# An up projection as one sequence of 77 products, with weight splits three products ahead and the convolution in pieces

## The chip, the core and the metric

The kernel runs on one NeuronCore of a Trainium2 chip. The metric is the device time of one execution in microseconds (us). "The time before" is the median of three executions; the profile is of one further execution. Engines are called as in the profile: PE is TensorE (PEld its weight loads), DVE is VectorE, ACT is ScalarE, POOL is GpSimd, SP is SyncE, which here only issues DMAs.

## The reference

One layer of a hybrid model on 512 tokens of width 1024: a mixer, a cross attention over 256 memory rows, and a feed-forward block with a short causal convolution. The change lies in the feed-forward block:

```python
def causal_dwconv(x, w, b):          # w has 3 taps here
    k_w = w.shape[0]
    s = x.shape[1]
    xp = jnp.pad(x, ((0, 0), (k_w - 1, 0), (0, 0)))
    y = b
    for j in range(k_w):
        y = y + xp[:, j:j + s] * w[j]
    return y

def conv_ffn(x, w_up, conv_w, conv_b, w_down):
    u = causal_dwconv(x @ w_up, conv_w, conv_b)
    gate, val = jnp.split(u, 2, axis=-1)
    return (jax.nn.gelu(gate) * val) @ w_down

def reference(x, mem, ...):
    ...
        x = layer_norm(ALPHA * x + mix, ln1_g[l], ln1_b[l])
        ca = memory_cross_attention(x, mem, ca_wq[l], ca_wkv[l], ca_wo[l])
        x = layer_norm(ALPHA * x + ca, ln2_g[l], ln2_b[l])
        ff = conv_ffn(x, ffn_w_up[l], ffn_conv_w[l], ffn_conv_b[l], ffn_w_down[l])
        x = layer_norm(ALPHA * x + ff, ln3_g[l], ln3_b[l])
```

`x @ w_up` is 512 x 1024 by 1024 x 5632; the 5632 outputs are 22 pairs of a gate tile and a value tile of 128 each.

## The kernel before

**Products.** Every float32 product is made of three matmuls (`mm3`, lines 154 to 157): each operand is split into a high half (`wh`, cast to fp32r on ACT, L125) and a low half (`wl`, the difference, on DVE, L126), and high x high, high x low and low x high are summed in PSUM. `split` (L119) makes both halves of 128 x 1024 weights, in four rotating `wh` and four rotating `wl` buffers.

**The up projection** goes by 11 "quads" (`quad`, L870) of two pairs each. A quad is a 2 x 2 block product of tokens (two halves of 256) by inputs (two halves of 512) and is done by Winograd's form of Strassen with seven products instead of eight. Each of them (`product`, L863) has 24 matmuls of 128 x 128 by 128 x 256. The token side (`forms`: A11, A12, S1 to S4, A22) is made once by `forms_block` (L794) for each of the four token blocks b, from transposes on PE (L801) and sums and splits on DVE and ACT; blocks 0 and 1 give A11 and A12 alone, the others need blocks 2 and 3 too. The weight side of a quad is made by DMA (`up_forms`, L844): blocks B11, B21, B22 are loaded on the SP queue (L851, L856), and sums are made by accumulating DMAs on the POOL queue (L848): B22 += B12; T1 = B11 + B12 (a load and an accumulation); B11 += the sum in B22; B21 += the sum in B11. B11, B21 and B22 are split as they are first, then added to, and the results are split again. Seven slots of 128 x 1024 hold these blocks.

From the third quad the order of products in a quad is S4 (of B22), A11 (B11), A12 (B21), S3 (B22 + B12), S2 (B11 + that), S1 (T1), A22 (B21 + that). Some PSUM results are kept by an ACT copy (L880: m1, m3, m7, u2), then added on DVE to a later bank (`put`, L884) into `uu`. When a quad's products are done its convolution follows for both pairs: per tile one `Identity` with bias and scale on ACT (L918) and two taps on DVE (L920), a Gelu on ACT (L922) and a multiply on DVE (L923) into `hf`.

**Around it.** The attention's output projection ends in a `slab` (L159, called at L824) that works block by block; `ln2_evict` (L819) adds the residual (L664, statistics L666), normalises (L670, L427, L677, L679) and returns the transposes of the block before. The first two quads begin with the products of A11 and A12 (L925 to L931): A11 and A12 of quad 0, then the transposes of block 3, then A11 and A12 of quad 1. Behind the up projection come two slabs of the down projection, whose left operand is split by `h_split` (L939).

**What sets the order.** Only the kernel's head is scheduled by hand (L279). Everywhere else a scheduler at build time puts the instructions into the in-order queues of the engines: an instruction goes when its inputs and a buffer are free by the scheduler's own reckoning, and among those that are free the one that stands first in the program text.

Of the kernel before, what the change touches and what calls it, by code (L numbers as in the profile page):

```python
# [40 lines left out]
def hybrid_block_kernel(  # L41
# [117 lines left out]
    def slab(xh, xl, w, c0, nk, evict, blocks=NB, late=0, mid=None, mid_k=4, halves=False, pre=None):  # L159
# [659 lines left out]
    def ln2_evict(b, ps):  # L819
        resid(b, ps, 512, 1024)  # L820
        norm(b)
        return lambda: forms_block(b)

    x2_last = slab(tok(oTh), tok(oTl), ca_wo[0], 512, KT, ln2_evict, late=4)  # L824
# [7 lines left out]

    hf = [raws[2]] + [H8(F32, "hf") for j in range(5)]
# [5 lines left out]
    blocks = [q2.tile([P, 1024], F32, name="rawx")]  # L839
    for _ in range(3):  # L840
        r = wp.tile([P, 2048], F32, name="raw", tag="raw", bufs=3)
        blocks += [r[:, 0:1024], r[:, 1024:2048]]

    def up_forms(q, order):  # L844
        blk = lambda kh, ch: ffn_w_up[q, kh, ch]
        at = {n: blocks[(4 * q + i) % 7] for i, n in enumerate(order + ("T1",))}
        r1, r2, r3, r4 = (at[n] for n in ("B11", "B22", "B21", "T1"))
        load, add = nc.sync.dma_start, lambda d, s_: nc.gpsimd.dma_start(d, s_, accum_op=OP.add)  # L848
        src = {"B11": blk(0, 0), "B22": blk(1, 1), "B21": blk(1, 0)}
        for n in order:  # L850
            load(at[n], src[n])  # L851
        for n in order:
            yield split(at[n], (8, P), 16)
            if n == "B22":
                add(r2, blk(0, 1))
        load(r4, blk(0, 0))  # L856
        add(r4, blk(0, 1))
        add(r1, r2)
        add(r3, r1)
        for r in (r2, r1, r4, r3):  # L860
            yield split(r, (8, P), 16)

    def product(bank, n, u, first, last):  # L863
        (h, l), (fh, fl) = u, forms[n]
# [5 lines left out]
    def quad(q):  # L870

        early = q < 2
        us = up_forms(q, ("B11", "B21", "B22") if early else ("B22", "B11", "B21"))
        uu = (hf[3 + q] if early else raws[q % 2]).rearrange("p (c j t) -> p c j t", c=2, j=2)
        g2 = lambda t: t.rearrange("p (j t) -> p j t", j=2)
        t1, t2_ = slice(0, 256), slice(256, 512)

        def kept(bank, name):
            t = t2(name)
            A.copy(t, bank)  # L880
            return g2(t)

        def put(dst, bank, other):
            V.tensor_tensor(dst, g2(bank), other, op=OP.add)  # L884

        def third():
            b = mx_bank()
            product(b, "S4", next(us), True, True)
            return kept(b, "m3")

        if not early:
            m3 = third()
        bp = mm_bank()
        product(bp, "A11", next(us), True, False)
        m1 = kept(bp, "m1")
        b = mx_bank()
        product(b, "A12", next(us), True, True)
        put(uu[:, 0, :, t1], b, m1)
        if early:
            yield  # L900
            m3 = third()
        b4 = mm_bank()
        product(b4, "S3", next(us), True, False)
# [25 lines left out]
    for g in early:  # L929
        for _ in g:  # L930
            pass  # L931
# [71 lines left out]
```

## Time and profile before

| | us |
|---|---|
| median of three executions | 874.77 (873.73 to 875.7) |
| profiled execution | 872.24 |
| its span, first to last instruction | 870.5 |
| PE busy | 806.2 (93%) |
| PEld busy | 709.3 (81%) |
| DVE busy | 570.4 (66%) |
| ACT busy | 376.3 (43%) |
| POOL busy | 68.3 (8%) |

Matmuls are pipelined, so a busy PE need not be a PE at its rate: the distance between the starts of two matmuls tells the rate. An engine's idle time counts only where a chain that sets the end goes through it. In the rows below, "x" is a count, and what stands in square brackets or after `<-` in a timeline is idle time before the instruction and what ended it.

### The profile page before, as it was taken

Reading aid. Unit: us, or ns where it says so; the run is one execution under the profiler, and the core shown is the slowest. Engines: PE = TensorE matmul, PEld = TensorE weight load, DVE = VectorE, ACT = ScalarE, POOL = GpSimd, SP = SyncE. Lnnn points to the kernel's source line nnn. Section 1 sums busy time; section 2 is a strip of 40 time slices with the busy share of each in tenths; the row PEclk is TensorE's granted clock in tenths of the full one; section 3 lists DMA queues with packets and bytes.
Section 4 is the critical chain, followed back from the end, with each engine's and each line's share of the span. In section 5 each row is a group of like instructions: output and inputs, shape, how many; then the busy total and the mean of one; then the engine's idle time right before and its main releaser. Section 6 shows DMA issues by size and latency. Waiting matters only on the chain. (4 is left out here: it accounts for less than half of the span.)

```text
span 870.5 us, 11772 instructions
## 1 busy us (share of the span) xinstructions
PE 806.2 (93%) x4696; PEld 709.3 (81%) x4696; DVE 570.4 (66%) x944; ACT 376.3 (43%) x512; POOL 68.3 (8%) x96
## 2 busy tenths in 40 slices
PE   9979999999999999999995778888898788999996
PEld 7858877787798888889884778888898788888885
DVE  6463498898783893385596377776666768934227
ACT  2289543553252052273152355555544557721110
POOL 1000001001100000000000111101111110000001
PEclk9989999999999999999998788999989899999999
DMA  9936742353257142313401777677686866422202
GB/s 263 184 75 168 105 77 45 91 125 105 79 203 258 48 145 98 97 63 132 121 2 25 184 191 161 158 174 172 152 187 171 194 150 161 173 97 97 73 1 98
DMA packets 53183, 111.05 MB, mean 128 GB/s; under 512 B 3844, under 2 KB 21380, under 8 KB 53128
## 3 DMA queue, kind: packets, MB, share of 16 engines
q1 hardware_dynamic: 46208, 84.58, 33.4%
q0 software_dynamic: 6336, 23.07, 14.3%
q10 hardware_dynamic: 584, 2.64, 0.9%
q8 instruction: 37, 0.61, 0.3%
q14 instruction: 18, 0.15, 0.1%
HBM read 96.63 MB, written 2.12 MB: 113 GB/s over the span
## 5 line engine op out<-in xcount | busy, mean ns | idle before, releaser
L126 DVE TENSOR_TENSOR wl<-raw,wh 128x1024 fp32r<-128x1024 f32 x155 | 187.4, 1221 | 172.3 <-ACT wh L125 171.6
L125 ACT CAST wh<-raw 128x1024 fp32r<-128x1024 f32 x155 | 161.7, 1051 | 311.3 <-PE mm L157 126.2
L157 PE MATMUL mm<-xf,wl 128*128 128x256 f32 x440 | 133.0, 303 | 32.2 <-DVE wl L126 32.1
L155 PE MATMUL mm<-xf,wh 128*128 128x256 f32 x440 | 133.4, 304 | 8.9 <-ACT wh L125 8.1
L156 PE MATMUL mm<-xf,wh 128*128 128x256 f32 x440 | 131.0, 299 | 0.0
L157 PEld LDWEIGHTS mm<-xf,wl 128*128 128x128 f32 x440 | 93.0, 211 | 35.0 <-DVE wl L126 35.0
L155 PEld LDWEIGHTS mm<-xf,wh 128*128 128x128 f32 x440 | 93.1, 212 | 11.4 <-ACT wh L125 8.7
L156 PEld LDWEIGHTS mm<-xf,wh 128*128 128x128 f32 x440 | 92.9, 211 | 0.0
L156 PE MATMUL mm<-wl,hTh 128*128 128x512 f32 (+1 forms) x180 | 65.9, 366 | 0.0
L155 PE MATMUL mm<-wh,hTh 128*128 128x512 f32 (+1 forms) x180 | 65.8, 366 | 0.0
L157 PE MATMUL mm<-wh,hTl 128*128 128x512 f32 (+1 forms) x180 | 65.8, 365 | 0.0
L155 PE MATMUL mm<-wh,xTh 128*128 128x512 f32 x128 | 52.5, 410 | 0.4 <-DVE xTh L285 0.4
L156 PE MATMUL mm<-wl,xTh 128*128 128x512 f32 x128 | 52.0, 406 | 0.0
L157 PE MATMUL mm<-wh,xTl 128*128 128x512 f32 x128 | 51.5, 402 | 0.0
L155 PE MATMUL mm<-xTh,wh 128*128 128x512 f32 x128 | 51.2, 400 | 0.0
L157 PE MATMUL mx<-xf,wl 128*128 128x256 f32 x176 | 49.4, 280 | 1.9 <-DVE wl L126 1.9
L156 PE MATMUL mm<-xTl,wh 128*128 128x512 f32 x128 | 51.1, 399 | 0.0
L157 PE MATMUL mm<-xTh,wl 128*128 128x512 f32 x128 | 51.0, 398 | 0.0
L156 PE MATMUL mx<-xf,wh 128*128 128x256 f32 x176 | 49.5, 281 | 0.8 <-DVE xf L247 0.8
L155 PE MATMUL mx<-xf,wh 128*128 128x256 f32 x176 | 49.9, 284 | 0.2 <-ACT wh L125 0.2
L920 DVE SCALAR_TENSOR_TENSOR fc<-xfr,ncols,fc 128x511 f32<-128x511 f32 (+1 forms) x36 | 25.0, 748 | 24.1 <-ACT fc L918 24.1
L155 PEld LDWEIGHTS mm<-wh,hTh 128*128 128x128 f32 x180 | 34.0, 189 | 5.6
(312 smaller groups left out, 1764.0 us busy)
## 6 DMA issues: line engine op xcount, KB each, us to landing
raw<-in_ffn_w_up_dram SPq DMA_DIRECT2D x37, 512.0 KB, 4.5
raw<-in_w_in_dram SPq DMA_DIRECT2D x14, 1024.0 KB, 8.4
raw<-in_ffn_w_down_dram SPq DMA_DIRECT2D x10, 1024.0 KB, 5.1
raw<-in_ffn_w_up_dram POOLq DMA_DIRECT2D x19, 512.0 KB, 8.6
raw<-in_ca_wkv_dram SPq DMA_DIRECT2D x8, 1024.0 KB, 5.3
raw<-raw POOLq DMA_DIRECT2D x15, 512.0 KB, 4.7
raw<-in_w_out_dram SPq DMA_DIRECT2D x4, 1024.0 KB, 8.9
raw<-in_ca_wq_dram SPq DMA_DIRECT2D x4, 1024.0 KB, 5.0
```

The lines of the kernel that those rows point to most:

```text
L125: A.copy(hv, src)
L126: V.tensor_sub(lv, src, f32(hv))
L155: T.matmul(ps, ah, bh, start=first, stop=False, skip_group_check=True)
L156: T.matmul(ps, ah, bl, start=False, stop=False, skip_group_check=True)
L157: T.matmul(ps, al, bh, start=False, stop=last, skip_group_check=True)
L920: V.scalar_tensor_tensor(f[:, d:], u[:, :S - d], w(2 - d), f[:, d:], op0=OP.mult, op1=OP.add)
```

## The change

The generators `quad` and `up_forms` are replaced by a list `seq` of 77 products (M1 to M7 stand for the forms A11, A12, S4, A22, S1, S2, S3) and a function `step` that places one of them. All six M1 and M2 products of quads 0 to 2 come first, then the others of quads 0 to 2 with the M3 of quad 3 among them, and from quad 3 on M1, M2, M7, M6, the next quad's M3, M5, M4. A step first places the PSUM copies and additions of the product before (`posts`), then the split of the product three places on (`split_of`) with the accumulating DMAs that follow from it, then loads that are due (`AHEAD`), then the 24 matmuls, then one of five pieces of a convolution. There are nine slots for weight blocks instead of seven, taken from a list of free ones; quad 0 has a spare block T3 = B22 + B12 with a load of its own. The first loads are placed inside the slab before (`ffn_begin`), the first three splits ahead of the last block's residual, the transposes of blocks 2 and 3 after the first and third steps. The first three splits of the down projection, each with its `h_split`, stand in the last three steps, and the remaining convolution pieces between the later units of that slab; the load of the last norm's weights moves from `mid_k` 4 to 12. The scheduler still chooses the order in the queues.

```diff
-    def slab(xh, xl, w, c0, nk, evict, blocks=NB, late=0, mid=None, mid_k=4, halves=False, pre=None):
+    def slab(xh, xl, w, c0, nk, evict, blocks=NB, late=0, mid=None, mid_k=4, halves=False, units=None):
...
-        for u in slab_units(w, c0, nk):
+        for u in units or slab_units(w, c0, nk):
...
-            if pre:
-                pre(k0)
...
+    h8 = [H8(F32, "hf") for j in range(5)]
+    hf = [raws[2]] + h8[1:] + h8[:1]
...
+    slots, free = [], list(range(9))
+
+    def ffn_begin():
+        half = lambda t: [t[:, 0:1024], t[:, 1024:2048]]
+        rt = [half(wp.tile([P, 2048], F32, name="raw", tag="raw", bufs=3)) for _ in range(3)]
+        slots[:] = rt[1] + rt[2] + [q2.tile([P, 1024], F32, name="rawx")] + rt[0] + half(hf[5])[::-1]
+        for q in range(3):
+            loads(q, ["B11", "B21"])
+        load(take(0, "T3"), blk(0, "B22"))
+        add(at(0, "T3"), blk(0, "B12"))
+        loads(0, ["B22"])
...
+    FORM = {"M1": "A11", "M2": "A12", "M3": "S4", "M4": "A22", "M5": "S1", "M6": "S2", "M7": "S3"}
+    seq = [(n, q) for q in range(3) for n in ("M1", "M2")]
+    seq += [(n, int(q)) for n, q in (w.split(".") for w in
+            "M3.0 M7.0 M6.0 M3.1 M5.0 M4.0 M3.2 M7.1 M6.1 M3.3 M5.1 M4.1 M7.2 M6.2 M5.2 M4.2".split())]
+    for q in range(3, NQ):
+        seq += [(n, q) for n in ("M1", "M2", "M7", "M6")] + [("M3", q + 1)] * (q + 1 < NQ) + [("M5", q), ("M4", q)]
...
+    def first_t(q):
+        loads(q, ["T1"])
+        add(at(q, "T1"), blk(q, "B12"))
+
+    def split_of(i):
+
+        n, q = seq[i]
+        src = {"M1": "B11", "M2": "B21", "M3": "B22", "M4": "B21", "M5": "T1", "M6": "B11", "M7": "B22"}[n]
...
+        units[i] = split(at(q, src), (8, P), 16)
+        t3 = "T3" if (q, "T3") in held else "B22"
+        if n == "M1":
+            if (q, t3) in held and (q, "summed") in units:
+                add(at(q, "B11"), at(q, t3))
+        if n == "M2":
+            if (q, "summed") in units:
+                add(at(q, "B21"), at(q, "B11"))
+        if n == "M3":
+            units[q, "summed"] = True
+            if t3 == "B22":
+                add(at(q, "B22"), blk(q, "B12"))
+            else:
+                drop(q, "B22")
+            if q not in (1, 2):
+                first_t(q)
+            if q < 3:
+                add(at(q, "B11"), at(q, t3))
+                add(at(q, "B21"), at(q, "B11"))
...
+    def conv_pieces(q):
+        y = {}
+
+        def taps(c, j):
...
+            A.activation(f, u, AF.Identity, bias=col(FCB + ft), scale=w(2))
+            if j:
+                A.activation(y[c, 0], y[c, 0], AF.Gelu_apprx_tanh)
+            for d in (1, 2):
+                V.scalar_tensor_tensor(f[:, d:], u[:, :S - d], w(2 - d), f[:, d:], op0=OP.mult, op1=OP.add)
+            y[c, j] = f
+
+        mul = lambda c: V.tensor_mul(hslice(2 * q + c), y[c, 0], y[c, 1])
+        return [lambda: taps(1, 0), lambda: taps(1, 1), lambda: (mul(1), taps(0, 0)), lambda: taps(0, 1),
+                lambda: mul(0)]
+
+    def step(i):
...
+        for f in posts:
+            f()
+        posts.clear()
+        if i + 3 < len(seq):
+            split_of(i + 3)
+        elif i + 3 - len(seq) < len(down_first):
+            down_first[i + 3 - len(seq)]()
+
+        for m, names in AHEAD.get(i, ()):
...
+        product(b, i, n in ("M1", "M2", "M3", "M7"), n in ("M2", "M3", "M4", "M5"))
+        if pieces:
+            pieces.pop(0)()
...
+    for q in range(1, NQ):
+        if q > 2:
+            AHEAD.setdefault(max(where["M3", q] - 8, 1), []).append((q, ["B22"]))
+            AHEAD.setdefault(where["M1", q] - 7, []).append((q, ["B11", "B21"]))
+    for i, w in ((3, (1, ["B22"])), (6, (2, ["B22"])), (7, (1, "T1")), (12, (2, "T1"))):
+        AHEAD.setdefault(i, []).append(w)
...
+    def ln2_evict(b, ps):
+        if b == NB - 1:
+            for i in range(3):
+                split_of(i)
+        resid(b, ps, 512, 1024)
+        norm(b)
+        return (lambda: forms_block(b)) if b < 2 else None
+
+    slab(tok(oTh), tok(oTl), ca_wo[0], 512, KT, ln2_evict, late=4, mid=ffn_begin)
+    step(0)
+    forms_block(2)
+    step(1)
+    step(2)
+    forms_block(3)
+    for i in range(3, len(seq)):
+        step(i)
...
     slab(tok(hTh), tok(hTl), ffn_w_down[0], 0, NPAIR, lambda b, ps: resid(b, ps),
-         mid=lambda: ln_load(ln3_g, ln3_b), pre=h_split)
+         mid=lambda: ln_load(ln3_g, ln3_b), mid_k=12, units=down_units())
```

## Rows read from the trace of the kernel before

**Rows 1.** The page, section 2: tenths of TensorE's granted clock in 40 slices

```profile
PEclk9989999999999999999998788999989899999999
```

**Rows 2.** Table of stages: length, busy time, granted clock, DMA share and rate

```profile
core 0: us, PE busy (x) PEld busy (x) DVE busy (x) ACT busy (x) POOL busy (x), PEclk, DMA share, GB/s
451.17:521.39 70.22, 51.13 (x347) 48.28 (x346) 43.22 (x60) 29.55 (x41) 8.79 (x10) 0.83 0.52 122
...
521.39:742.51 221.12, 193.18 (x1515) 189.44 (x1513) 158.40 (x193) 122.20 (x159) 29.39 (x34) 0.92 0.71 169
742.51:870.50 127.99, 120.88 (x596) 102.48 (x594) 63.81 (x89) 29.55 (x31) 3.69 (x4) 0.98 0.25 87
```

**Rows 3.** Timeline of PE in the third quad: start, duration, line, operation, tiles

```profile
527.85 0.28 PE L155 MATMUL mx<-xf,wh 128*128 128x256 f32 x1
...
529.55 0.28 PE L155 MATMUL mm<-xf,wh 128*128 128x256 f32 x1
...
533.01 0.58 PE L157 MATMUL mm<-xf,wl 128*128 128x256 f32 x1 [3.07 <-DVE wl L126]
```

**Rows 4.** Waits in the nine late quads: total us, times, longest

```profile
PE mm L157 <- DVE wl L126: 27.3, 9, 4.5
DVE fc L920 <- ACT fc L918: 27.2, 9, 4.4
...
DVE wl L126 <- ACT wh L125: 16.3, 15, 2.2
```

**Rows 5.** Timeline of DVE in the third quad

```profile
526.46 2.78 DVE L920 SCALAR_TENSOR_TENSOR fc<-hf,ncols,fc 128x511 f32<-128x511 f32 x4 [3.02 <-ACT fc L918]
...
530.42 1.40 DVE L920 SCALAR_TENSOR_TENSOR fc<-hf,cols,fc 128x510 f32<-128x510 f32 x2
531.74 1.22 DVE L126 TENSOR_TENSOR wl<-raw,wh 128x1024 fp32r<-128x1024 f32 x1
```

**Rows 6.** Timeline of ACT in the third quad

```profile
524.65 1.05 ACT L125 CAST wh<-raw 128x1024 fp32r<-128x1024 f32 x1 [3.37 <-DMA raw<-in_ffn_w_up_dram]
525.61 1.52 ACT L918 ACTIVATE fc<-hf,cols,ncols 128x512 f32<-128x512 f32 x2
```

**Rows 7.** Timeline of DVE at the opening of the up projection

```profile
449.97 1.22 DVE L126 TENSOR_TENSOR wl<-rawx,wh 128x1024 fp32r<-128x1024 f32 x1
...
452.84 0.68 DVE L811 TENSOR_TENSOR xfr<-mx,xfr 128x512 f32<-128x512 f32 x1
453.44 0.68 DVE L813 TENSOR_TENSOR xfr<-xfr 128x512 f32<-128x512 f32 x1
```

**Rows 8.** Timeline of PE at the opening: the transposes of blocks 2 and 3

```profile
450.38 1.03 PE L801 MATMUL mx<-ident,xres 128*128 128x128 f32 x8
...
463.02 1.64 PE L801 MATMUL mx<-ident,xres 128*128 128x128 f32 x8 [3.08 <-DVE xres L679]
```

**Rows 9.** DMA view of the late quads: queues' shares; issues, median us to landing

```profile
q0 software_dynamic: 5016, 18.25, 44.2%
q1 hardware_dynamic: 6022, 18.89, 26.7%
...
raw<-raw POOLq DMA_DIRECT2D x13, 512.0 KB, 4.7
```

**Rows 10.** DMA view of 610 to 622 us, four issues together

```profile
raw<-in_ffn_w_up_dram SPq DMA_DIRECT2D x2, 512.0 KB, 9.6
raw<-in_ffn_w_up_dram POOLq DMA_DIRECT2D x2, 512.0 KB, 9.4
```

**Rows 11.** DMA view of 472 to 479 us, one accumulation from DRAM

```profile
raw<-in_ffn_w_up_dram POOLq DMA_DIRECT2D x1, 512.0 KB, 5.7
```

**Rows 12.** Timeline of POOL in a late quad

```profile
598.69 0.87 POOL L848 DMA_DIRECT2D rawx<-raw  x1 [8.93 <-issue]
...
610.67 0.85 POOL L848 DMA_DIRECT2D raw<-in_ffn_w_up_dram  x1 [5.97 <-DMA raw<-in_ffn_w_up_dram]
```

**Rows 13.** Timeline of DVE beside that issue

```profile
609.36 2.36 DVE L126 TENSOR_TENSOR wl<-raw,wh 128x1024 fp32r<-128x1024 f32 x2
```

More of the change, by code (lines that the diff above doesn't have):

```diff
@@ L844, in up_forms @@
[L844 to L861, printed above, removed]
@@ new lines, in hybrid_block_kernel, with take, drop, loads @@
+    held, units = {}, {}
+    def take(q, n):
+        ok = [f for f in free if not (q >= NQ - 2 and 5 <= f < 7) and not (q >= 7 and f == 8)]
+        held[q, n] = ok[0]
+        free.remove(ok[0])
+        return slots[ok[0]]
+    at = lambda q, n: slots[held[q, n]]
+    def drop(q, n):
+        free.append(held.pop((q, n)))
+    def loads(q, names):
+        for n in names:
+            load(take(q, n), blk(q, n if n != "T1" else "B11"))
+    def first_t(q):
+        loads(q, ["T1"])
+        add(at(q, "T1"), blk(q, "B12"))
@@ L865, in product @@
+    def product(bank, i, first, last):
+        (h, l), (fh, fl) = units.pop(i), forms[FORM[seq[i][0]]]
         for j in range(2):
@@ L868, in product @@
                     first and j == 0 and k == 0, last and j == 1 and k == 3)
[L870 to L903, printed above, removed]
-        m7 = kept(b4, "m7")
-        product(bp, "S2", next(us), False, False)
-        u2 = kept(bp, "u2")
-        product(bp, "S1", next(us), False, True)
-        put(uu[:, 1, :, t1], bp, m3)
-        put(uu[:, 1, :, t2_], bp, m7)
-        product(b4, "A22", next(us), False, True)
-        put(uu[:, 0, :, t2_], b4, u2)
-        for c in (1, 0):
-            y = []
-            for j in range(2):
-                ft = j * NPAIR + 2 * q + c
-                u, f = uu[:, c, j, :], t2("fc")
-                w = lambda i: ncols[:, i * 44 + ft:i * 44 + ft + 1] if c else col(FCW + i * 44 + ft)
-                A.activation(f, u, AF.Identity, bias=col(FCB + ft), scale=w(2))
-                for d in (1, 2):
-                    V.scalar_tensor_tensor(f[:, d:], u[:, :S - d], w(2 - d), f[:, d:], op0=OP.mult, op1=OP.add)
-                y.append(f)
-            A.activation(y[0], y[0], AF.Gelu_apprx_tanh)
-            V.tensor_mul(hslice(2 * q + c), y[0], y[1])
@@ L925, in hybrid_block_kernel, with keep, put @@
-    early = [quad(q) for q in range(2)]
-    next(early[0])
-    x2_last()
-    next(early[1])
-    for g in early:
-        for _ in g:
-            pass
-    for q in range(2, NQ):
-        for _ in quad(q):
-            pass
+    banks, kept, uus, posts, pieces = {}, {}, {}, [], []
+    g2 = lambda t: t.rearrange("p (j t) -> p j t", j=2)
+    def keep(q, name, bank):
+        t = t2(name)
+        A.copy(t, bank)
+        kept[q, name] = g2(t)
+    def put(q, c, half, bank, name):
+        V.tensor_tensor(uus[q][:, c, :, half * 256:(half + 1) * 256], g2(bank), kept[q, name], op=OP.add)
@@ L950, in h_split, with down_unit, down_units @@
         V.tensor_sub(hTl[j][:, s], hf[j][:, s], f32(hTh[j][:, s]))
+    down = slab_units(ffn_w_down[0], 0, NPAIR)
+    early_units = []
+    def down_unit():
+        h_split(2 * len(early_units))
+        early_units.append(next(down))
+    down_first = [down_unit] * 3
+    def down_units():
+        yield from early_units
+        for k in range(6, NPAIR, 2):
+            h_split(k)
+            if pieces:
+                pieces.pop(0)()
+            yield next(down)
+    def ln2_evict(b, ps):
[13 more added lines that the diff above has]
+        step(i)
+    for f in posts:
+        f()
     slab(tok(hTh), tok(hTl), ffn_w_down[0], 0, NPAIR, lambda b, ps: resid(b, ps),
-         mid=lambda: ln_load(ln3_g, ln3_b), pre=h_split)
+         mid=lambda: ln_load(ln3_g, ln3_b), mid_k=12, units=down_units())
     def ln3_evict(b, ps, cs):
```

56 lines of the change are left out of this document (44 added, 12 removed).

## The prediction

> **What bounds the kernel now.** I read the page's slices first, then the stages, then one product, then the queues that it waits for. In the slices of 21.8 us, the digit of TensorE's clock is below 9 in the third and then only in slices 22 to 25, 30 and 32, which all lie in the up projection, the stage that the change rewrites [rows 1]. The table of stages gives its size: 70.22 us for the first two quads (14 products) and 221.12 us for the other nine (63 products), with a mean granted clock of 0.83 and 0.92, a mixture of the two levels 1.2 and 2.4 GHz; the down projection behind it runs at 0.98 [rows 2].
>
> What would the stage cost without waits? In an undisturbed product, fifteen matmuls take 529.55 - 527.85 = 1.70 us, 0.1133 us each, so a product of 24 takes 2.72 us [rows 3], a quad of seven 19.0 us, and 77 products 209.4 us. The stage takes 291.3 us, so 81.9 us are lost: 221.1 - 63 x 2.72 = 49.7 us in the nine late quads (5.5 us each) and 70.2 - 38.1 = 32.1 us in the opening.
>
> The late loss sits at one place. The fourth product of a quad (S3) starts two matmuls and then stops for `wl`, the low half of its split: in the quad shown for 3.07 us [rows 3]; over the nine quads TensorE waits there 27.3 us, in nine stops [rows 4]. The remaining 22.4 us are mostly matmuls at the lower clock behind each such stop. Why is that `wl` late? On DVE it starts at 531.74, behind seven convolution taps and a multiply, the first of which began at 526.46 [rows 5]; `wh` of the same split was already cast at 524.65, after 3.37 us in which ACT stood at the head of its queue for a DMA, with the four `Identity` operations of the convolution behind it [rows 6]. So ACT waits for the accumulated block B22 + B12, the convolution of the quad before waits for ACT, and the split waits for the convolution. DVE is not short of time as such: 158.4 of 221.1 us, 17.6 us a quad [rows 2].
>
> **The change, part by part.** *Convolution in pieces, splits three products ahead.* Instructions are the same in number. Removed is the order: the convolution of quad q stood in the text ahead of the S3 split of quad q+1; now each step first places the PSUM evictions, then the split of the product three on, then one fifth of the convolution. Four `wh`/`wl` buffers let that split start when the product before the present one has ended, and it must be done three products later: 8.16 us, of which it needs 1.05 + 1.22 us [rows 5, 6]. So 5.9 us are in hand. The whole convolution costs DVE 8 x 0.67 + 2 x 0.60 = 6.6 us (four taps in 2.78 us [rows 5], multiplies at the 0.60 us spacing of [rows 7]), one piece 1.3 to 1.9 us. What hides the convolution is TensorE's own products; without that cover it costs what it costs now, 5.5 us a quad. The scheduler may still let pieces run ahead of a split that is not ready; a whole burst of 6.6 us exceeds what is in hand by only 0.7 us.
>
> *DMAs moved.* Per quad there are, as before, four loads on SP and four accumulations on POOL (plus one load for a spare block in quad 0). Together they hold the sixteen DMA engines 44.2 + 26.7% of 221.1 us, 17.4 us a quad, some of it early down weights [rows 9]; this is under 19.0. What matters is the order on POOL, an in-order queue: B22 += B12 now stands five steps (13.6 us) ahead of its split, formerly three, so the wait at ACT goes. Behind it on POOL stands T1 += B12, which waits for T1's load; behind that B11 += B22 and B21 += B11. The chain that closes on itself is: split of M3 (2.3 us), B22 += B12 lands, B11 += B22 lands, split of M6, and 1 us later the next M3's split on the same queues. The first addition lands in 5.7 us when little else moves [rows 11] and 9.4 us when four issues crowd [rows 10], the second in 4.7 us [rows 9]: a period of 13.7 to 17.4 us, hidden under 19.0 by at least 1.6. SP's queue gains no wait that lasts: following the list of free slots through the sequence, nearly every load goes into a slot whose last reader is three or more steps old (in the first quads a load of B22 and one of T1 wait for a split just placed).
>
> *Opening.* All six products that need the first two token blocks alone now run before the first that needs blocks 2 and 3 (formerly three, and TensorE stopped 3.08 us for the last block's normalisation [rows 8]). From 450.38 TensorE has 6 x 2.72 + 2 x 0.79 us (the eight transposes of [rows 8], until 451.17) = 17.9 us of work, to 468.3. DVE has, from 449.97 to the seventh product: 7 splits x 1.14 [rows 13] and 21 operations of 0.60 us (one residual, four passes of the norm, nine and five for the forms, two evictions) [rows 7], with about 1.2 us (estimate) of small ones: 21.8 us, to 471.8, and about 1 us for hand-overs. So the seventh product starts near 472.8, 4.5 us late; with 2.5 us for the low clock behind it (22.4 / 9) and 1.6 us of transposes the opening costs 8.6 us over pure products. Bounds of the stop: 0, if splits slip ahead of 449.97, and 10, if the norm is again scattered among the forms.
>
> *First quads.* M3 of quads 0 to 3 come only three products apart, so their additions crowd on POOL: three a quad, 5.7 + 4.7 + 4.7 = 15.1 us if alone, 18.8 at the crowded landing. They fit in 16.3 us or miss by 2.5 a quad; the bounds are 0 and 15 us, I take 5, nearer the lone addition.
>
> *Late quads.* 55 products, 7.86 quads, lose between 0 and today's 5.5 us each. I take 0.8, near zero since the split has 5.9 us in hand: 6.3 us. ACT's copy of `u2` now has the next quad's M3 beside it.
>
> *Down projection.* Its first three splits and `h_split`s move into the last three steps; each unit has 24 matmuls of cover, and the bound is 0 to 3 us. I take 0.
>
> Sum: 450.38 + 209.4 + 8.6 + 5 + 6.3 = 679.7 instead of 742.51, 62.8 us earlier. The profiled execution took 872.24 us (1.7 over its span of 870.5): 809.4. The median of the three runs is 2.5 us above that execution, so I forecast **812**.
>
> **A rule weighed.** While DVE ran two splits back to back from 609.36 [rows 13], POOL issued an addition at 610.67 in 0.85 us; with DVE idle, at 598.69, it took 0.87 [rows 12]. So POOL was not held up. The Trainium skill, "SBUF — State Buffer", section "SBUF: two separate sides", says that a DVE operation with two SBUF inputs can hold a port pair against a GpSimd operation that reads SBUF for its whole length; the trace disagrees for these issues. As a mechanism here: each of the two additions of the chain would wait for one 1.22 us split, the period would be 17.4 + 2.4 = 19.8 us, 0.8 over the products, some 8 us on ten rounds: 820. I give it 0.03.
>
> **The rivals.** (a) *DVE becomes the bound.* It has 17.6 of 19.0 us to do, and today it waits for ACT 27.2 us before taps and 16.3 us before `wl` [rows 4], 4.8 us a quad. From a third of this on it is the bound (19.2); if all of it stays, its period is 22.4: 3.4 x 7.86 = 26 us less the 6 counted, 832. Against it: half of the waiting is the DMA wait at ACT that goes.
>
> (b) *The pieces do not stay pieces.* The scheduler is free in its order and the change does not do what it says: the burst still stands ahead of a split, and 5.5 us a quad stay: 43 - 6 = 37 us more, 849. Against it: splits now come ahead in the text, where ties are decided.
>
> (c) *No change*, if DMA and order together restore both losses: 0.03.
>
> (d) *Slower: T1's addition ahead of B22's on POOL.* If the free order puts T1 += B12 first, the chain begins with T1's load. At the crowded landings this is 9.6 + 9.4 + 4.7 + 1 = 24.7 us a round [rows 9, 10], eleven rounds from 472.8, and 5.4 us of products behind: 750, 7.4 us later than now, and with the first quads' 5 us 12.4 later: 887. It decides from a period of 23.6 us, (742.5 - 5.4 - 472.8 - 5) / 11. With the addition uncrowded (5.7) it is hidden as long as the load lands within 7.6 us (7.6 + 5.7 + 4.7 + 1 = 19.0). For it: the opening's crowding; against it: B22's addition is earlier in the text and its wait is shorter.
>
> **How the numbers follow.** Forecast 0.56 (800 to 822; all free, 798), port rule 0.03, (a) 0.14, (b) 0.15, (c) 0.03, (d) 0.09. For 8 in 10 the range goes from 798 to 850. Its lower end is the sum with the opening's stop, first quads and late quads near their lower bounds. What a measurement can tell from no change is about 0.2%, 1.7 us: faster 0.88, same 0.03, slower 0.09.
>
> **What would show it.** Right: the wait of `mm L157` for `wl` shrinks from 27.3 us to a few, the clock of the late quads is near 1.00, a quad takes 19 to 20 us, DMA engines are busy over 80% there, and the seventh product starts within a few us of 472. Wrong: a stop at the same place in every quad, with taps ahead of `wl` on DVE (b); DVE without idle time while TensorE waits (a); ACT waiting for a DMA at M6's cast, with POOL held by T1's load (d).

## The result, and the profile after

The changed kernel takes 827.97 us (median of four runs, 824.04 to 830.77), the kernel before, run beside it, 875.24 us: a ratio of 0.9459, 95% interval 0.9417 to 0.9501. Forecast were 812 us and a range of 798 to 850. The direction was right, and so was the mechanism in the main; the time is 16 us above the forecast and lies between the forecast's own range (800 to 822) and rival (a).

The profiled execution took 830.77 us. Its stages, in the columns of [rows 2]: the first 22 products, the next 49 (seven quads), the last six, the down projection.

```profile
core 0: us, PE busy (x) PEld busy (x) DVE busy (x) ACT busy (x) POOL busy (x), PEclk, DMA share, GB/s
452.01:527.35 75.34, 67.62 (x545) 65.96 (x544) 60.04 (x79) 43.69 (x59) 13.71 (x16) 0.95 0.78 191
527.35:674.21 146.86, 137.89 (x1178) 136.69 (x1177) 124.28 (x154) 94.00 (x123) 23.43 (x27) 0.99 0.78 188
674.21:701.12 26.91, 19.39 (x146) 18.90 (x145) 18.66 (x24) 14.39 (x18) 0.86 (x1) 0.81 0.56 144
701.12:829.10 127.98, 120.88 (x596) 102.52 (x594) 63.25 (x88) 28.85 (x30) 3.69 (x4) 0.98 0.26 87
```

The up projection takes 249.1 us instead of 291.3, the down projection the same 127.98 us. Cut at the same counts of products (24 matmuls each), the stage before had 98.5, 171.4 and 21.5 us. So the first 22 products gained 23.1 us, the seven quads 24.5 us (a quad 20.98 us instead of 24.5; pure products are 19.04), and the last six lost 5.4 us. The digits of TensorE's clock, to be held against [rows 1], show the same: below 9 only in the third slice, in the one where the last quad lies, and in the last.

```profile
PEclk9989999999999999999999999999999997999998
```

The wait of `mm L157` for `wl`, 27.3 us in [rows 4], is gone. These stand in its place (same columns, the 55 products from 527.35 on):

```profile
DVE wl L126 <- ACT wh L125: 27.4, 15, 4.1
ACT wh L125 <- DMA raw<-raw: 13.8, 5, 4.5
...
PE mm L155 <- ACT u L919: 9.6, 7, 3.0
...
PE mm L155 <- ACT m L919: 6.9, 1, 6.9
...
ACT wh L125 <- DMA raw<-rawx: 6.2, 2, 4.9
...
ACT wh L125 <- DMA rawx<-hf: 5.8, 1, 5.8
ACT wh L125 <- DMA raw<-hf: 4.8, 1, 4.8
...
ACT wh L125 <- DMA hf<-raw: 4.6, 1, 4.6
```

TensorE now waits for ACT's copies (`u2`, once `m7`), 16.5 us in eight stops; ACT in turn waits at the head of its queue for accumulated blocks, and DVE waits for ACT. One late quad, quad 6, shows the chain (timelines of POOL, ACT, DVE and PE; in brackets the idle time before and who ended it):

```profile
588.49 0.87 POOL L843 DMA_DIRECT2D raw<-in_ffn_w_up_dram  x1 [8.19 <-DMA raw<-in_ffn_w_up_dram]
589.14 1.12 POOL L843 DMA_DIRECT2D raw<-hf  x1
...
596.38 1.05 ACT L125 CAST wh<-raw 128x1024 fp32r<-128x1024 f32 x1 [4.76 <-DMA raw<-hf]
...
597.46 1.22 DVE L126 TENSOR_TENSOR wl<-raw,wh 128x1024 fp32r<-128x1024 f32 x1 [3.64 <-ACT wh L125]
...
605.34 0.63 ACT L934 ACTIVATE fc<-fc 128x512 f32<-128x512 f32 x1 [1.45 <-DVE fc L936]
605.88 1.03 ACT L125 CAST wh<-raw 128x1024 fp32r<-128x1024 f32 x1
606.82 0.57 ACT L919 COPY u<-mm 128x512 f32<-128x512 f32 x1
...
607.45 0.38 PE L155 MATMUL mm<-xf,wh 128*128 128x256 f32 x1 [1.07 <-ACT u L919]
```

POOL issues T1 += B12 once T1's load has landed, and 0.65 us behind it B11 += B22. (By the slots that the later casts read, this T1 is quad 7's: the scheduler has drawn its load and its addition forward.) M6's cast needs B11 += B22 and starts 7.24 us after its issue; ACT stands there for 4.76 us with `Identity`, copies and other casts behind it. DVE idles 3.64 us for that cast; it has 17.8 us of work in a quad (124.28 us in seven), so it can make good little in the 19.04 us of a quad's pure products. The backlog does not clear within the quad: the Gelu waits for a tap that DVE did late, and `u2`'s copy comes behind it at 606.82, although M6's last matmul had begun at 603.26. M5 needs that bank and stops TensorE.

The other late quads bear this out in part. T1's addition stands just ahead of B11's in five of eight (3 to 6 and 10), and there B11 += B22 lands 7.1 to 7.4 us after its issue. In quads 7 and 8 nothing is issued just ahead, it lands after 4.6 and 4.5 us, and quad 8 is the only one of the seven without a loss (19.04 us). But in quad 9 it takes 7.0 us with no other addition issued in the 9.5 us before: T1's addition is not the only thing that can delay it.

### The profile page after: what moved, and what is told of

Its sections match the earlier page's. It is cut to its first block, busy times and chain, and to the rows that moved or that the text cites. A ratio compares the mean times of both kernels' runs of the same rounds, so it can differ in the third digit from the quotient of the medians.

```text
span 829.1 us, 11747 instructions
## 1 busy us (share of the span) xinstructions
PE 785.2 (95%) x4696; PEld 691.3 (83%) x4696; DVE 569.6 (69%) x944; ACT 375.1 (45%) x512; POOL 68.4 (8%) x96
## 5 line engine op out<-in xcount | busy, mean ns | idle before, releaser
L126 DVE TENSOR_TENSOR wl<-raw,wh 128x1024 fp32r<-128x1024 f32 x141 | 171.3, 1220 | 173.9 <-ACT wh L125 173.3
L125 ACT CAST wh<-raw 128x1024 fp32r<-128x1024 f32 x141 | 147.4, 1050 | 255.8 <-PE mm L157 122.7
L155 PE MATMUL mm<-xf,wh 128*128 128x256 f32 x440 | 126.0, 287 | 20.9 <-ACT u L919 13.4
L156 PE MATMUL mm<-xf,wh 128*128 128x256 f32 x440 | 124.9, 284 | 1.0 <-DVE xf L245 1.0
L157 PE MATMUL mm<-xf,wl 128*128 128x256 f32 x440 | 124.3, 283 | 0.0
L155 PEld LDWEIGHTS mm<-xf,wh 128*128 128x128 f32 x440 | 85.3, 194 | 23.2 <-ACT u L919 15.2
L156 PEld LDWEIGHTS mm<-xf,wh 128*128 128x128 f32 x440 | 85.3, 194 | 1.4 <-DVE xf L245 1.4
L157 PEld LDWEIGHTS mm<-xf,wl 128*128 128x128 f32 x440 | 85.4, 194 | 0.3 <-DVE wl L126 0.3
L157 PE MATMUL mm<-wh,hTl 128*128 128x512 f32 (+1 forms) x180 | 65.8, 366 | 0.0
L157 PE MATMUL mm<-wh,xTl 128*128 128x512 f32 x128 | 50.8, 397 | 0.7 <-DVE xTl L285 0.6
L157 PE MATMUL mm<-xTh,wl 128*128 128x512 f32 x128 | 51.2, 400 | 0.0
L157 PE MATMUL mx<-xf,wl 128*128 128x256 f32 x176 | 49.6, 282 | 0.0
L426 POOL TENSOR_TENSOR lnrs<-lnrs,neghalf 128x1 f32<-128x1 f32 x12 | 11.2, 931 | 344.8 <-DVE lnrs L425 344.8
```

The lines of the kernel that those rows point to most:

```text
L125: A.copy(hv, src)
L126: V.tensor_sub(lv, src, f32(hv))
L155: T.matmul(ps, ah, bh, start=first, stop=False, skip_group_check=True)
L156: T.matmul(ps, ah, bl, start=False, stop=False, skip_group_check=True)
L157: T.matmul(ps, al, bh, start=False, stop=last, skip_group_check=True)
L426: G.tensor_tensor(out_, out_, neghalf[:, 0:n], op=OP.pow)
```

## The experiments

The stages of each kernel are read from one execution. Four executions of the changed kernel lie 6.7 us apart, so a difference of a few us between the stages of two kernels shows nothing by itself.

Theory 1: the late stops come from B11 += B22 landing late, because T1's addition is issued right ahead of it. Theory 2: ACT's order (Gelu and a cast ahead of `u2`'s copy) makes them by itself. Theory 3, rival (a) of the prediction: DVE is the bound. Ratios are to the kernel before, with 95% intervals; "changed kernel" is the 828 us one.

**T1's addition behind B11's.** For quads 3 to 10 only:

```
 if n == "M1":
     if (q, t3) in held and (q, "summed") in units:
         add(at(q, "B11"), at(q, t3))
+    if q > 2: first_t(q)
 if n == "M3": ...
-    if q not in (1, 2): first_t(q)
+    if q == 0: first_t(q)
```

> Changed kernel, but in quads 3 to 10 T1's load and its addition are issued behind B11 += B22 (at the split of M1) instead of ahead of it (at the split of M3). Theory 1 (the stops in front of M5 come from B11 += B22 landing late, 7.1 us instead of some 4.7, because T1's addition is issued right ahead of it and shares the DMA engines; ACT stands at M6's cast for it and everything behind it on ACT is late): B11's addition lands in 4.5 to 5.7 us, ACT's waits for DMAs at wh L125 in the up stage (16.0 + 9.2 + 5.8 us in the changed kernel) fall below 10 us, a late quad takes 19.0 to 19.8 us instead of 21, and the time is 814 to 820 us instead of 828. Theory 2 (ACT's order, with Gelu and a cast ahead of u2's copy, makes the stop by itself): the cast no longer waits, but quads stay at 20.5 to 21 and the time at 825 to 829. Theory 3 (DVE is the bound at 17.3 us a quad plus hand-overs): no change, 826 to 830.

Measured: 818.49 us, 0.9342 (0.9317 to 0.9368), as theory 1 had it. Its table of stages for the seven quads, and timelines of POOL and ACT in one of them:

```profile
522.24:661.27 139.03, 137.66 (x1179) 137.25 (x1177) 124.85 (x154) 94.83 (x123) 24.15 (x28) 1.00 0.85 198
...
577.50 0.86 POOL L843 DMA_DIRECT2D hf<-raw  x1 [8.54 <-DVE wl L126]
580.91 0.87 POOL L843 DMA_DIRECT2D hf<-in_ffn_w_up_dram  x1 [2.54 <-DMA hf<-in_ffn_w_up_dram]
...
582.81 1.05 ACT L125 CAST wh<-hf 128x1024 fp32r<-128x1024 f32 x1 [1.17 <-DMA hf<-raw]
```

Issue to cast is 5.31 us instead of 7.24, ACT waits 1.17 us instead of 4.76, and seven quads take 139.0 us (19.9 each) with TensorE's clock at 1.00. One expectation missed: ACT's DMA waits in the stage did not fall under 10 us (9.5 + 9.4 + 6.6 + 6.4 us are its largest). Most of them no longer reach TensorE. The built order follows the edit only in part: in quads 4 to 8 B11's addition has none just ahead of it and lands 4.5 to 5.2 us after its issue, but in quads 9 and 10 the scheduler put T1's ahead of it again, and it lands after 7.8 and 7.3 us.

**ACT in the order of the text** from M1 of quad 3 on:

```
+    with tc.manual_schedule(engines={mybir.EngineType.Activation}):
         for i in range(where["M1", 3], len(seq)): step(i)
```

> Changed kernel, but from M1 of quad 3 on ACT's instructions stand in the order of the text: the copies of a product's bank ahead of the cast of the split three on, one Gelu a piece. The additions and their order on POOL stay. Theory 1 (late landing of B11 += B22 holds ACT at M6's cast): ACT stands there as before (16 us and more of DMA waits at wh L125), u2's copy is some 1 to 2 us earlier behind it, and of the 12 to 14 us of stops in front of M5 at most 6 go: 822 to 829 us; more if the fixed order makes a copy or a Gelu wait for DVE. Theory 2 (the order alone): the stops in front of M5 go though the cast still waits, 814 to 818. Theory 3 (DVE): 826 to 830.

Measured: 831.73 us, 0.9495 (0.9466 to 0.9524), 2.7 us above the range of theory 1. ACT's order alone brings nothing, but theory 2 isn't cleanly excluded by it, as ACT's timeline in the same quad as above shows:

```profile
597.22 1.05 ACT L125 CAST wh<-raw 128x1024 fp32r<-128x1024 f32 x1 [6.72 <-DMA raw<-hf]
...
607.31 0.63 ACT L934 ACTIVATE fc<-fc 128x512 f32<-128x512 f32 x1 [1.82 <-DVE fc L936]
607.85 0.57 ACT L919 COPY u<-mm 128x512 f32<-128x512 f32 x1
```

The cast waits as before, and in this order too a Gelu that waits for DVE stands ahead of `u2`'s copy. An order in which the copy passes the Gelu wasn't tried.

**T1's additions left out** in quads 3 to 10 (M5 there lacks B12's part):

```
 def first_t(q):
     loads(q, ["T1"])
-    add(at(q, "T1"), blk(q, "B12"))
+    if q < 3: add(at(q, "T1"), blk(q, "B12"))
```

> Changed kernel without the additions T1 += B12 from DRAM in quads 3 to 10 (eight transfers of 512 KB left out; M5 of these quads lacks B12's part); loads, splits and the rest stay. Theory 1: B11 += B22 lands in 4.5 to 5 us, no DMA wait at M6's cast, quads of 19.0 to 19.5 us, 812 to 817. If this is 4 us or more below the run with T1's addition moved behind B11's, then the total load of the DMA engines counts and not only the order. Theory 2: 825 to 829. Theory 3 (DVE): 826 to 830.

Measured: 807.7 us, 0.9227 (0.9201 to 0.9252), 4 us and more below every expectation. The table of stages, seven quads and the last six products:

```profile
522.66:655.94 133.28, 133.28 (x1178) 133.28 (x1177) 124.25 (x153) 95.16 (x123) 18.07 (x21) 1.00 0.74 183
655.94:677.85 21.91, 18.20 (x147) 17.81 (x145) 18.85 (x24) 14.50 (x18) 0.86 (x1) 0.92 0.50 138
```

49 products in 133.28 us are 2.72 us each: TensorE never stops, while DVE does all its work (124.25 of 133.28 us). That ends theory 3. The run is 10.8 us below the one with the additions moved (5.7 us in the seven quads, 4.0 us in the last six). By my expectation this would show that their load on the DMA engines counts beside their place; the rows don't bear that out. Here are a quad of this run and then two of the run with the additions moved:

```profile
598.82:617.86 19.04, 19.04 (x170) 19.04 (x169) 17.30 (x22) 13.28 (x17) 2.58 (x3) 1.00 0.71 167
...
601.90:621.70 19.80, 19.80 (x171) 19.80 (x170) 17.31 (x22) 13.27 (x17) 2.77 (x4) 1.00 0.77 180
...
543.44:562.57 19.13, 19.13 (x170) 19.12 (x169) 18.83 (x25) 13.77 (x18) 3.44 (x4) 1.00 0.95 227
```

TensorE has no idle time in any of them and a granted clock of 1.00, yet the second quad is 0.76 us longer: its matmuls start 0.118 us apart instead of 0.113. That distance holds through four whole quads and parts of others of the run with the additions moved and makes 3.8 of the 5.7 us; it does not go with the DMA engines' share, since the third quad, at 0.95, has 0.113. What sets it is open. In the last six products, T1's addition stood ahead of B11's again in the other run. So no run here shows a price of the additions' load by itself.

**The convolution at once** behind a quad's last product, splits three ahead kept:

```
-    if pieces:
+    while pieces:
         pieces.pop(0)()
```

> Changed kernel with one part undone: the five pieces of a quad's convolution are all placed in the step behind its last product, splits stay three products ahead. It weighs pieces against distance. By my prediction's sum a burst of 6.6 us on DVE exceeds the 5.9 us in hand by 0.7 us a quad: 828 + 5 to 8, so 830 to 838. If the pieces are what brought the gain, the old loss of 5.5 us a quad is back: 855 to 870. If DVE is the bound anyway (theory 3), its order is indifferent: 826 to 830.

Measured: 824.32 us, 0.9416 (0.9389 to 0.9444): no slower than with pieces, and outside the 830 to 838 of my sum. The seven quads even take 138.5 us instead of 146.9. But the built order of POOL differs here: in quads 4 to 9 B11 += B22 goes ahead of T1's addition, in quad 6 by 2.67 us (timeline of POOL):

```profile
586.45 0.86 POOL L843 DMA_DIRECT2D raw<-hf  x1 [5.59 <-DVE wl L126]
589.12 0.88 POOL L843 DMA_DIRECT2D raw<-in_ffn_w_up_dram  x1 [1.81 <-DMA raw<-in_ffn_w_up_dram]
```

So this run changed two things. The run to hold it against is the one with T1's addition behind B11's, which keeps the pieces: 139.0 us there. In the seven quads the pieces bring nothing, and the order on POOL shows again; the first 22 products took 77.9 us here, 72.5 there.

**Splits two ahead** instead of three (loads keep their distance to the splits):

```
-    if i + 3 < len(seq): split_of(i + 3)
+    if i + 2 < len(seq): split_of(i + 2)
```

> Changed kernel with one part undone: a split is placed two products ahead of its own instead of three (and loads placed ahead keep their distance to the splits); pieces and sequence stay. My prediction put what is in hand at 8.16 - 2.3 = 5.9 us with three ahead; with two it is 3.1 us, less than a landing that is 2.4 us late plus the copies in front of it. If the distance is what brought the gain in the late quads: 840 to 855, with stops for wl or wh in each quad. If the order on POOL (B22's addition earlier) brought it and the distance is spare: 826 to 832.

Measured: 832.54 us, 0.9529 (0.9498 to 0.9559), at the upper edge of what I expected if the distance is spare. The seven quads take 146.8 us, as with three; the difference lies in the first 22 products, 81.9 us instead of 75.3 (in the profiled execution, with 837.46 us the longest of the four).

**The old opening**: M3 of quad 0 as the fourth product in the text:

```
-seq = [(n, q) for q in range(3) for n in ("M1", "M2")]
+seq = [("M1", 0), ("M2", 0), ("M1", 1), ("M3", 0), ("M2", 1), ("M1", 2), ("M2", 2)]
```

> Changed kernel with one part undone: M3 of quad 0, which needs the forms of all four token blocks, is again the fourth product, ahead of M2 of quad 1 and M1 and M2 of quad 2. By my prediction the start of the seventh product in the changed kernel is set by DVE (471.8 + 1, measured 475.3), so M3.0 starts at the same time and the three products pushed behind it cost their 8.2 us: 835 to 838. Rival: the time until M3.0's forms shrinks when splits of fewer products stand ahead of them on DVE (three splits of 1.14 us and two evictions): cost 3 to 5 us, 831 to 833.

Measured: 833.02 us, 0.9524 (0.9499 to 0.9549); the first 22 products take 82.2 us, 6.8 more. Here too the scheduler did not keep to the text: M1 of quad 2 ran ahead of M3, so two products were pushed behind it, not three; and M3.0 started 21.9 us after the stage's first matmul instead of 23.3, its forms being ready a little sooner, as the rival had it (its 831 to 833 just holds).

**M3 late**: M3 of the next quad behind M5 and M4 again:

```
-seq += [(n, q) for n in ("M1", "M2", "M7", "M6")] + [("M3", q + 1)] * (q + 1 < NQ) + [("M5", q), ("M4", q)]
+seq += [(n, q) for n in ("M1", "M2", "M7", "M6", "M5", "M4")] + [("M3", q + 1)] * (q + 1 < NQ)
```

> Changed kernel with one part undone: in the late quads M3 of the next quad comes behind M5 and M4 again instead of ahead of them; splits three ahead and pieces stay. The chain from M3's split over B22 += B12 and B11 += B22 to M6's split then has 4 products (10.9 us) instead of 6 (16.3 us), and M5 follows directly on M6 with u2's copy between. If the place of M3 is what brought most of the gain of the late quads: ACT stands at M6's cast for 3 us and more in every quad, 850 to 870. If it is spare, since three splits in advance cover it: only the copy of u2 shows, about 1.2 us a quad, 833 to 840.

Measured: 850.35 us, 0.9714 (0.9688 to 0.974), at the lower edge of what I expected if M3's place counts. In the seven quads (24.1 us each) TensorE waits for copies behind an ACT that waits for two additions in a row (waits of that stretch; ACT's timeline):

```profile
PE mm L155 <- ACT m L919: 25.1, 11, 3.9
...
600.17 1.05 ACT L125 CAST wh<-hf 128x1024 fp32r<-128x1024 f32 x1 [5.33 <-DMA hf<-in_ffn_w_up_dram]
605.34 1.05 ACT L125 CAST wh<-raw 128x1024 fp32r<-128x1024 f32 x1 [3.41 <-DMA raw<-hf]
```

**No split ahead and the convolution at once**, M3 early (the loads keep their distance to the splits, and the first three units of the down projection go back behind the up projection):

```
-    if i + 3 < len(seq): split_of(i + 3)
+    if i + 0 < len(seq): split_of(i + 0)
-    if pieces:
+    while pieces:
```

> Changed kernel with two parts undone at once: each split stands in the text at its own product (none ahead) and the five pieces of the convolution come at once behind a quad's last product; the sequence of products stays. Pieces alone cost nothing when undone, one step less of advance 4.5 us. If these two cover for each other, undoing both brings back the stop of some 5 us a quad for wl behind the convolution: 860 to 875. If neither is what brought the gain, because the scheduler hoists splits by itself as far as the four buffers allow: 835 to 848.

Measured: 850.95 us, 0.9727 (0.969 to 0.9765), between the two expectations. Here the old wait for `wl` of [rows 4] is back, with 2.0 us a stop instead of 3.0 (seven quads of 23.2 us; waits of that stretch, and one stop in PE's timeline):

```profile
PE mm L157 <- DVE wl L126: 14.3, 7, 2.3
...
592.79 0.58 PE L157 MATMUL mm<-xf,wl 128*128 128x256 f32 x1 [2.31 <-DVE wl L126]
```

**All three undone**, by the edits of the two runs above together; the order of the opening is kept:

> Changed kernel with all three parts undone in the late quads: M3 behind M4, no split ahead, convolution at once; the opening (six products ahead of the first M3) stays. If the parts cover for each other: late quads of 24 to 25 us as in the kernel before, 865 to 880. If they add up singly (each alone costs what its own run shows): the sum of the runs with M3 late and with the other two parts undone, 840 to 860.

Measured: 850.68 us, 0.9711 (0.968 to 0.9743). This lies in the range that I gave for parts that add up, but by luck: the losses of the two runs above, 22.4 and 23.0 us, would add up to 873. The parts neither add up nor bring the old quads back. The three totals near 850 are alike, their parts are not (first 22 products, last 55):

| kernel | first 22 us | last 55 us |
|---|---|---|
| before | 98.5 | 192.9 |
| all three undone | 87.1 | 179.6 |
| no split ahead, burst | 85.7 | 184.1 |
| M3 late | 74.1 | 195.9 |
| changed kernel | 75.3 | 173.8 |

In the first 22 the splits ahead and the pieces together are worth some 10 us. In the last 55 the early M3 without them (184.1) and they without the early M3 (195.9) are no better than neither (179.6); only both together are (173.8): additions early and splits early are one condition. (The splits were never put back without the pieces; that the pieces bring nothing there is from the run with the convolution at once.)

**The end.** In the kernel with T1 behind B11 (818 us) the largest loss left in the late products is one stop ahead of the last two, M5 and M4 of quad 10 (timelines of POOL, ACT and PE, then the table of stages for the last six products):

```profile
657.14 0.88 POOL L843 DMA_DIRECT2D hf<-in_ffn_w_up_dram  x1 [8.05 <-DMA hf<-in_ffn_w_up_dram]
657.79 1.12 POOL L843 DMA_DIRECT2D rawx<-raw  x1
665.72 0.86 POOL L843 DMA_DIRECT2D raw<-rawx  x1 [6.81 <-DMA rawx<-raw]
...
674.42 1.04 ACT L125 CAST wh<-raw 128x1024 fp32r<-128x1024 f32 x1 [4.84 <-DMA raw<-rawx]
...
677.89 0.58 PE L155 MATMUL mm<-xf,wh 128*128 128x256 f32 x1 [5.16 <-ACT m L921]
...
661.27:687.14 25.87, 20.14 (x147) 19.64 (x145) 18.63 (x24) 14.38 (x18) 0.86 (x1) 0.87 0.58 151
```

T1's addition of quad 10 (657.14) stands just ahead of B11's here again. B11's lands after 7.3 us, and only then can B21 += B11 be issued. The cast for M4 stands on ACT for the latter until 8.70 us after its issue; the copies of `m7` and `u2` that the last two products need stand behind it. Two edits were made on this kernel. First, another order of the last two quads (M3 of quad 10 two products earlier; M7 between M6 and M5):

```
+        if q < NQ - 2:
 ...
+    seq += [(n, int(q)) for n, q in (w.split(".") for w in
+            "M1.9 M2.9 M3.10 M7.9 M6.9 M1.10 M5.9 M4.9 M2.10 M6.10 M7.10 M5.10 M4.10".split())]
-and not (q >= 7 and f == 8)]
+and not (7 <= q < NQ - 2 and f == 8)]
```

(The last two lines give quad 10 one half buffer more, which the order needs.)

> The kernel with T1's addition behind B11's, and besides another order of the last two quads: M3 of quad 10 two products earlier, M1 of quad 10 ahead of M5 and M4 of quad 9, and M7 between M6 and M5 of quad 10, so that its chain of three additions has ten products from M3's split to M4's (27 us) instead of eight (22 us), and the copies of the last quad have a product beside them. In the kernel without this order the end loses 5.4 us in one stop ahead of M5.10 and about 3.4 us of low clock behind it, because ACT stands at M4.10's cast until B21 += B11 has landed. If the chain of additions is what ends last there: the stop falls below 1 us and the time by 6 to 9 us, to 810 to 812. Rival: the end is bound by the 1 MB loads of down weights and the casts of hTh that stand beside it: then the stop only moves and the time falls by 0 to 3 us, 815 to 818.

Measured: 809.01 us, 0.925 (0.9214 to 0.9286), 1 us below what I expected; the last six products take 17.2 us, the stop is 0.9. Second, the slots' rule that frees half buffers for early down loads dropped:

```
-ok = [f for f in free if not (q >= NQ - 2 and 5 <= f < 7) and not (q >= 7 and f == 8)]
+ok = [f for f in free]
```

> The kernel with T1's addition behind B11's, and besides the rule dropped that keeps three half buffers free of blocks from quads 7 and 9 on, so that the first loads of down weights (1 MB each) start later and share less with the last additions. If these loads are what makes B21 += B11 of quad 10 land in 8.6 us: it lands in 5 to 6 us and the stop ahead of M5.10 shrinks from 5.4 to 2 to 3 us; but the first down products then wait for their weights, so the time is 815 to 824. If the loads don't matter for it: landing 8 us or more, time 816 to 826.

Measured: 808.99 us, 0.9244 (0.9222 to 0.9265), a gain where I expected about none (timelines of POOL and ACT):

```profile
651.10 0.88 POOL L843 DMA_DIRECT2D hf<-in_ffn_w_up_dram  x1 [2.69 <-DVE wl L126]
659.90 0.85 POOL L843 DMA_DIRECT2D raw<-hf  x1 [7.92 <-DVE wl L126]
665.07 0.86 POOL L843 DMA_DIRECT2D raw<-raw  x1 [4.31 <-DVE xfr L925]
...
664.53 1.05 ACT L125 CAST wh<-raw 128x1024 fp32r<-128x1024 f32 x1 [1.25 <-DMA raw<-hf]
```

B22's, B11's and B21's additions of quad 10 stand 8.8 and 5.2 us apart, B11's is cast 4.63 us after its issue, and the last six products take 17.1 us. The edit did two things at once. T1's load of quad 10 found a slot a quad sooner, so its addition (638.92) stands 0.71 us ahead of quad 9's B11 += B22, which lands after 7.2 us, and no longer ahead of quad 10's. And no 1 MB load ran beside B21's. Which of the two counted more stays open; the down projection did not wait for its weights.

**Both end edits together** (the other order of the last two quads, and the rule dropped):

> The kernel with T1's addition behind B11's, with the other order of the last two quads and without the rule that keeps half buffers free for early down loads: both gained 9.5 us alone over the 818.5 us of the first. If they take away the same stop at the end (5.4 us and the low clock behind it): no sum, 806 to 810. If the late loads help the late quads by something else: 801 to 805.

Measured: 807.59 us, 0.9231 (0.9171 to 0.9291): no sum, since both take away the same stop. TensorE stays busy through the whole end, and what is left above pure products is 13.6 us in the first 22 and 5.9 us in the seven quads, 2.5 us of the latter by matmuls 0.118 us apart (table of stages):

```profile
450.16:523.62 73.46, 66.93 (x546) 65.53 (x544) 59.92 (x78) 43.95 (x59) 12.85 (x15) 0.95 0.80 199
523.62:662.83 139.21, 136.54 (x1178) 136.03 (x1177) 124.27 (x152) 94.86 (x123) 25.06 (x29) 1.00 0.87 199
662.83:679.79 16.96, 16.96 (x146) 16.96 (x145) 16.92 (x21) 14.86 (x18) 0.00 (x0) 1.00 0.58 188
```

The three kernels at the end, 807.6 to 809.0 us, beat both the kernel before and the changed one; between themselves their intervals don't tell them apart.

## Why the prediction was right or wrong

The sum forecast 809.4 us for the profiled execution; it took 830.8. The 21.4 us by its terms:

| term of the sum | predicted us | measured us |
|---|---|---|
| start of the up projection | 450.38 | 452.01 |
| 22 products beyond 59.9 (opening 8.6, first quads 5) | 13.6 | 15.5 |
| 55 late products beyond 149.5 | 6.3 | 24.2 |
| down projection | 0 | 0 |

*Start:* 1.6 us that are not the change's; in the other kernels here the same work ahead of it ends between 448.8 and 452.0.

*Opening and first quads:* right. M3 of quad 0, the seventh in the list, starts at 475.27, 23.3 us after the first product, where the sum had 22.4; TensorE's halts before it are 1.03 + 0.60 + 1.89 us (with four matmuls of M7 of quad 0 drawn ahead between them), where 4.5 were taken. The first nine products lose 8.2 us (8.6 taken) and the next thirteen 7.3 (5 taken). That the 5 came so near is partly luck: the 16.3 us that I set against the additions of the first quads are six products, where I had just put the M3s three apart. Undoing this part cost 6.8 us in the first 22 products.

*Late quads:* the mis-sized term, 17.9 of the 21.4 us: 13.6 in the seven quads (1.9 each instead of 0.8) and 10.6 in the last six products. The step that failed is the chain, "hidden by at least 1.6". I compared its period with a quad's 19.0 us, and took the second landing as 4.7 us from [rows 9]. The period does fit. But B11 += B22 can't be issued before M1's split has read the raw block, whatever B22 does, and from that split to M6's are three products, 8.16 us: not a period but a delay, into which 2.3 us of split and a landing must fit. With 4.7 us it would, by 1.1 us; with T1's addition issued just ahead it takes 7.2 and doesn't. The order T1, B11 on POOL stood in my own text ("behind that B11 += B22"), with B11's price taken from rows where it stood alone. That the T1 in front of it is mostly the next quad's, drawn forward by the scheduler, I had not foreseen. Moving T1 brought that cast to 5.3 us behind the issue and the quad to 19.9; leaving T1's addition out, 19.04.

*ACT's copy of `u2`:* I gave it the next M3 as cover and asked only whether its product had ended. In the quad shown it was late because ACT, an in-order queue, had stood at a cast and still had a backlog, with a Gelu that waited for DVE ahead of the copy. What this order of Gelu and copy costs by itself is open. The same holds for the end, which I took as late quads like the others: no next M3 stands between the last additions, M6 and M5 follow on each other, T1's addition is again just ahead of B11's (670.44 and 671.09), and the stop of 7.2 us is the largest of the stage.

*The gain of the late quads:* the reason was named rightly (B22's addition earlier, splits ahead; two products ahead did as well as three there), but one part was credited wrongly. I had the pieces hide the convolution, with only 0.7 us short for a whole burst; undone alone, they cost nothing in the seven quads (138.5 us beside 139.0 with the same order on POOL). And M3's place and the splits ahead have no price each in the late products: one without the other is worth nothing there.

*The rivals.* (a) fell: with T1's additions out, DVE does the same work in quads of 19.04 us. (b) fell as a case of its own: a burst doesn't stop TensorE while splits stand ahead; only without them does the wait for `wl` return (14.3 us). (d) came in one quad alone (quad 9: T1's addition at 640.35, B22's at 640.97), but its mechanism, T1's addition ahead of another on POOL, is what took most of the missing gain of the seven quads: 8.0 us were missing, and moving it gave back 7.8; I had looked at it only ahead of B22's addition, the first of the chain, not of B11's, the second. The port rule did not show: POOL issued its additions in 0.84 to 0.89 us all through the late quads, 1.06 to 1.14 where one was issued right behind another.

*What would show it.* The wait for `wl` went, clock 0.99; quads of 19 to 20 us did not come (20.98). DMA engines busy over 80% was wrong: 0.78, since the stretch was longer; with T1 moved it is 0.85.

*Still open.* With all three parts undone the kernel is still 24 us faster than before. Its first 22 products take 87.1 us instead of 98.5 and its seven quads 160.1 instead of 171.4. The opening, the nine slots with other load distances and the order that the scheduler then finds are left as causes; no run here tells them apart.

## What to carry to other kernels

A chain of transfers that closes on itself must be checked twice: its period against the loop's, and each link's delay from the instruction that releases it to the one that needs it. A landing time from rows where a transfer runs alone isn't its price right behind another one; look at what the same queue issues just before. And where an in-order engine stands for a transfer, everything behind it in its queue is late too, so the stop shows up under another name (`u2`), on work that needs nothing of the transfer; undo parts one at a time and together, and compare them stage by stage, before any of them gets the credit.

## What the runs showed of the hardware

Of two additions of 512 KB issued 0.65 us apart (588.49 and 589.14) the first lands as if it were alone, the second 2.5 us behind it (DMA view of these two issues, us to landing):

```profile
raw<-in_ffn_w_up_dram POOLq DMA_DIRECT2D x1, 512.0 KB, 5.3
raw<-hf POOLq DMA_DIRECT2D x1, 512.0 KB, 7.1
```

With nothing issued just ahead, B11 += B22 lands after 4.5 to 5.2 us in quads 4 to 8 of the kernel with T1 moved. One addition's packets keep the sixteen DMA engines busy for 2.7 us (63.6% of 4.2 us in the second view below), about the 2.5 us by which the second is later: an estimate that fits packets moved one addition after the other.

A second fact is the distance between matmuls: 0.113 us or 0.118 us, for whole products on end, at a granted clock of 1.00 in both cases and without idle time. It made 3.8 us in the seven quads of one kernel (139.0 us) and nothing in those of another (133.28 us), so it has to be taken out before such stages are compared.

More surprising is an addition issued just behind a 1 MB load on the other queue. In the kernel with T1 moved, SP issues the load at 665.19 and POOL the addition at 665.72. The DMA views of 665.7 to 670.2 us and of 670.2 to 674.4 us (packets, MB, share of 16 engines) show that the addition moves nothing until the load is nearly done:

```profile
q1 hardware_dynamic: 473, 0.97, 86.0%
...
q0 software_dynamic: 144, 0.52, 63.6%
q1 hardware_dynamic: 55, 0.08, 5.1%
```

In the changed kernel it looks the same: the load is issued at 678.57 and the addition at 679.09, 12 packets of the addition move before 684.0 and 100 from there to 686.0, and ACT's cast on it starts at 688.73, 9.6 us after the issue. The Trainium skill, "DMA: Bandwidth & Descriptors", section "Queues, rings and completion order", says that each DMA engine takes turns between the queues that have work, packet by packet; by that the two would have shared the time from the start. The trace shows one after the other; whether the addition's descriptors came late or the engines held them back, no run here tells.
